# Which projections fill the waits of a delta-rule mixer: v's block before the banded attention, z's block in the scan

## The chip, the core and the metric

The kernel runs on one core of a Trainium2 chip. The metric is the device time of one execution in microseconds (us). Of the core's engines five appear below: TensorE (PE in the rows), VectorE (DVE), ScalarE (ACT), GpSimd (POOL) and SyncE (SP), which issues the loads.

## What the kernel computes

The program holds two blocks of a network for 256 tokens of width 1024, and the change lies in the first mixer of the second block. That mixer works on 272 rows (16 learned rows ahead of the 256 tokens, `N2` in the kernel). It projects them with one matrix, gives one part to a delta-rule mixer that runs over the sequence in both directions, and one part to a banded attention of 8 heads. Cut to what matters:

```python
def ab_mixer(u, w_in, ...):
    proj = u @ w_in
    qa, ka, va, za, ba, aa, qb, kb, vb = split_cols(proj, AB_SIZES)
    ya = delta_mixer(qa, ka, va, za, ba, aa, ...)
    yb = window_mixer(rmsnorm(qb), rmsnorm(kb), vb, sink)
    return concatenate([ya, yb]) @ w_out

def delta_mixer(hq, hk, hv, hz, hb, ha, conv_w, ...):
    q, k, v = split_cols(silu(centred_conv(concatenate([hq, hk, hv]), conv_w)), ...)
    q, k = l2norm(q), l2norm(k)                 # beta, g: gates of both directions
    fwd = gated_delta_chunked(q, k, v, beta_fwd, g_fwd)
    bwd = rev(gated_delta_chunked(rev(q), rev(k), rev(v), ...))
    return rmsnorm(fwd + bwd, o_gain) * silu(hz)

def gated_delta_chunked(q, k, v, beta, g):
    a_mat = where(strict, (k * beta) @ k.T * decay, 0)      # per chunk and head
    sol = triangular_solve(a_mat, [v * beta, k * beta * exp(gc)], unit_diagonal=True)
    def step(s, xs):                                        # the scan over chunks
        v_new = u_n - w_n @ s
        o = q_n @ s + qk_n @ v_new
        s = s * gl_n + k_n.T @ v_new
        return s, o
```

So v is wanted by the scan and not before it, and z only after the scan, in the last product. The triangular solve needs q, k and the gates, neither v nor z.

## The kernel before, in words

All work of the mixer is on one core. The 4 heads of the delta rule have keys and values of width 128; the sequence is cut into three pieces (16, 128 and 128 rows), and both directions run side by side. `delta` has four stages one after the other:

- the side rounds (`side`, L1575 to L1622): the norms of q and k, then `prepare`, which builds the decay masks, the scaled products and the rows of the gates for each piece and direction;
- the levels (`levels`): the triangular systems are inverted by doubling. `blocks` does four levels of 32x32 products (L1639), with a copy on ACT, a subtraction and a 32x32 transpose on DVE after each; `pairs` joins blocks to 64 and to 128 (L1678, L1685, L1688, L1695, L1700);
- the scan (`scan`, L1762 to L1801): three steps in each direction, matmuls of 128 columns with a copy or a product on ACT, POOL or DVE between them;
- `finish` (L1810, L1813), which norms the result and multiplies it by z; then the output projection.

Each stage is a chain over several engines, so PE would wait in it. The kernel therefore has filling work, written as a generator `fill`, and `spread(stage, fill, share)` takes `share` steps of it after each step of the stage: `SF` in the side rounds, `LF` in the levels, `CF` in the scan. What is left is run after the scan. The filling work consists of

- projections (`rest`): a block is 128 columns of the matrix over 272 rows. Its weights are split into a high and a low part (`wsplit`: a copy on ACT at L236, a subtraction on DVE at L267), and 24 matmuls of 272 columns follow (L272, L273, L274). Blocks 8 to 11 are v, 12 to 15 are z, 19 and 20 belong to the banded attention. A block of v ends in a short convolution (`conv_late`: L1314, L241 and four times L245 on DVE), a block of z in one product (L1395);
- the silu of v or z (`silu_exp`: three steps on ACT and one, L1307, on POOL) and `turned(vn, v)`, which transposes v by 12 matmuls (L297);
- the banded attention (`window`): two units for the learned rows and 16 of the heads (8 heads, two pieces of the rows; a head below is one such unit). It is a score (L1491, two records in the trace), a softmax on DVE and ACT, three transposes (L297) and products with the values (L1507).

The text of the program doesn't fix the order on an engine: a scheduler places the instructions from the order in which they are written, their costs and what they wait for. The rows of the section on the change are what it put out for either kernel.

Of the kernel before, what the change touches and what calls it, by code (L numbers as in the profile page):

```python
# [33 lines left out]
MORE = 2  # L34
PD = 2
PF = 5
LF = 4
WD = 2
SF = 1
CF = 4  # L40
VS = 0.7
WP = ()
ND = 2
OVER_AT = 4
# [102 lines left out]
def run(gen, n=None):  # L147

    while n is None or n > 0:
        if next(gen, gen) is gen:  # L150
            return
        n = None if n is None else n - 1
# [7 lines left out]
def spread(gen, fill, share):  # L160

    due = 0
    for _ in gen:
        due += share
        run(fill, int(due))
        due -= int(due)
# [14 lines left out]
class Kern:  # L181
# [1333 lines left out]
    def delta(self, c1, p1, pw, qk, v, z, qw, vba, rest, norms, qw_norms):  # L1515
# [38 lines left out]
        def turned(dst, x):  # L1554
            for t in (1, 2, 0):
                cc = self.hcols(t)
                n = cc.stop - cc.start
                b = self.bank()
                for h in range(4):
                    self.transpose(b[:n, h * 128:(h + 1) * 128], x[:, h, cc])  # L1560
                nc.scalar.copy(dst[:n, t], b[:n])
                yield
# [141 lines left out]
        def levels():  # L1704
            def through(d):
                yield from blocks(d)
                yield from pairs(d)

            return in_turn([through(0), through(1)])

        def side():
            yield from norms
            yield from flow([prepare(1, 0), prepare(1, 1), turned(kn, qk[:, 4:8])], PD)
            yield from flow([prepare(t, d) for t in (2, 0) for d in range(2)], PD)

        side = side()
        def values():
            yield from rest(pw, [8, 9, 10, 11])
            for h in range(4):
                self.silu_exp(pw, v[:, h], v[:, h])  # L1720
                yield
            yield from turned(vn, v)

        def filling():
            yield from rest(pw, [19, 20, 12, 13, 14, 15])
            yield from qw_norms(pw)
            due = 0
            for _ in self.window(c1, p1, pw, qw, vba, y):
                yield
                due += VS  # L1730
                while due >= 1:
                    run(vs, 1)
                    due -= 1
                    yield
            for h in range(4):
                self.silu_exp(pw, z[:, h], z[:, h])
                yield

        vs = values()
        y, fill = p1.tile([128, 4, N2], F32, name="yw"), filling()  # L1740
        spread(side, fill, SF)
        spread(levels(), fill, LF)
        run(vs)
        oT = v
        seen, st = set(), [None, None]
        def scan(step, d):
# [551 lines left out]
```

## Time and profile before

| | |
|---|---|
| median of 3 runs | 1607.31 us (1604.68 to 1607.84) |
| the profiled execution | 1608.48 us, of which the span of the profile is 1606.7 us |
| busy in the span | PE 1535.0, DVE 824.1, ACT 645.3, POOL 201.0 us |
| side rounds, last 44 us (917.0 to 961.4) | PE 42.73, DVE 33.62 us busy |
| levels (961.4 to 1017.7) | PE 50.40 of 56.3 us busy |
| scan (1017.7 to 1090.2) | PE 33.87 of the first 38.3 us, 34.18 of the other 34.2 us |

Times of stages are counted from the span's start. The granted clock is a column of the views: 1.00 is the upper level of TensorE's clock (2.4 GHz), 0.50 the lower one (1.2 GHz). A matmul at the lower level takes up to about twice as long, and PE then counts as busy for longer with the same work: a busy PE says nothing of its pace.

### The profile page before, as it was taken

The page shows a single profiled execution, that of the slowest core. Times are in us where ns is not written, and L with a number is a line of the kernel's source. Part 1 is how long each engine was busy: PE and PEld are TensorE (multiplying, and loading weights), DVE is VectorE, ACT ScalarE, POOL GpSimd, SP SyncE. Part 2 cuts the span into 40 slices and gives each one's busy share as a digit, 9 for nine tenths or more (in the row PEclk, how much of TensorE's full clock was granted, in tenths as well). Part 3 has the DMA queues.
Part 4 walks back from the last instruction along what each step waited for, and adds up shares of the span by engine and source line. Part 5 has one row for each costly group of instructions (what it writes and reads, how often), then busy time and mean ns, then how long its engine had stood idle before and what let it go on. Part 6 is the DMA issues. An engine that isn't in the chain of part 4 may idle for free.

```text
span 1606.7 us, 26861 instructions
## 1 busy us (share of the span) xinstructions
PE 1535.0 (96%) x10998; PEld 1170.3 (73%) x10998; DVE 824.1 (51%) x1624; ACT 645.3 (40%) x1309; POOL 201.0 (13%) x236
## 2 busy tenths in 40 slices
PE   7999999989799999998997899899999999999999
PEld 7788744444287876454436787588999998799998
DVE  6677612212345772131216776536666666576665
ACT  5466411111136642110115674545444455554443
POOL 0130100000101001000003631301111023220000
PEclk9999999999999999999999999689999999999999
DMA  8335899999462489999943111025555452254540
GB/s 348 140 131 186 338 407 421 380 421 421 145 239 71 159 315 356 422 382 419 421 206 140 66 54 56 1 83 191 173 184 184 157 192 79 79 180 164 184 156 27
DMA packets 50034, 348.77 MB, mean 217 GB/s; under 512 B 5616, under 2 KB 6896, under 8 KB 8688
## 3 DMA queue, kind: packets, MB, share of 16 engines
q1 hardware_dynamic: 49904, 346.97, 56.2%
q8 instruction: 90, 1.47, 0.4%
q14 instruction: 40, 0.33, 0.1%
HBM read 345.90 MB, written 1.05 MB: 216 GB/s over the span
## 4 chain that ended last, share of the span: by engine, by line
PE 45%; DVE 4%; ACT 2%; POOL 1%; issue 1%; DVEq 0%; POOLq 0%; ACTq 0%
PE bank L274 10%; PE bank L272 10%; PE bank L273 10%; PE bank L1033 3%; PE bank L1067 2%; DVE ring L267 1%; PE aux L1507 1%; PE aux L297 1%; PE bank L994 1%; PE aux L1491 1%; PE aux L2008 1%; PE bank L1639 1%; ACT ring L236 1%; PE bank L1769 1%; PE aux L1986 1%
## 5 line engine op out<-in xcount | busy, mean ns | idle before, releaser
L236 ACT ACTIVATE ring<-ring 128x1024 fp32r<-128x1024 f32 (+3 forms) x188 | 185.8, 994 | 188.6 <-PE bank L274 166.6
L267 DVE TENSOR_TENSOR ring<-ring,ring 128x1024 fp32r<-128x1024 f32 x145 | 180.4, 1244 | 93.5 <-ACT ring L236 93.1
L272 PE MATMUL bank<-uh,ring 128*128 128x272 f32 (+1 forms) x744 | 218.6, 294 | 2.3 <-ACT ring L236 2.3
L274 PE MATMUL bank<-uh,ring 128*128 128x272 f32 (+1 forms) x744 | 215.5, 290 | 4.2 <-DVE ring L267 3.7
L273 PE MATMUL bank<-ul,ring 128*128 128x272 f32 (+1 forms) x744 | 215.0, 289 | 0.0
L274 PEld LDWEIGHTS bank<-uh,ring 128*128 128x128 f32 x744 | 141.4, 190 | 6.0 <-DVE ring L267 5.6
L272 PEld LDWEIGHTS bank<-uh,ring 128*128 128x128 f32 x744 | 141.3, 190 | 5.1 <-ACT ring L236 2.5
L273 PEld LDWEIGHTS bank<-ul,ring 128*128 128x128 f32 x744 | 141.2, 190 | 0.9 <-issue 0.2
L274 PE MATMUL bank<-rh,ring 128*128 128x272 f32 (+1 forms) x496 | 141.6, 286 | 0.0
L272 PE MATMUL bank<-rh,ring 128*128 128x272 f32 (+1 forms) x496 | 141.4, 285 | 0.0
L273 PE MATMUL bank<-rl,ring 128*128 128x272 f32 (+1 forms) x496 | 140.9, 284 | 0.0
L1039 DVE TENSOR_TENSOR hid<-hid,bank 128x512 f32<-128x512 f32 x16 | 11.0, 687 | 186.4 <-PE bank L1033 173.7
L273 PEld LDWEIGHTS bank<-rl,ring 128*128 128x128 f32 x496 | 93.8, 189 | 0.0
L272 PEld LDWEIGHTS bank<-rh,ring 128*128 128x128 f32 x496 | 93.2, 188 | 0.0
L274 PEld LDWEIGHTS bank<-rh,ring 128*128 128x128 f32 x496 | 93.0, 187 | 0.0
L267 POOL TENSOR_TENSOR ring<-ring,ring 128x1024 fp32r<-128x1024 f32 x6 | 14.5, 2436 | 574.4 <-ACT ring L236 574.4
L1257 POOL TENSOR_TENSOR fr<-fr 128x272 f32<-128x272 f32 (+1 forms) x64 | 40.2, 629 | 287.3 <-DVE fr L245 283.4
L245 DVE SCALAR_TENSOR_TENSOR big<-bank,gs,big 128x512 fp32r<-128x512 f32 x32 | 24.0, 750 | 99.2 <-ACT big L236 97.5
L267 DVE TENSOR_TENSOR ring<-wsp,ring 128x1024 fp32r<-128x1024 f32 x41 | 52.8, 1287 | 26.1 <-ACT ring L236 26.1
L236 ACT ACTIVATE ring<-wsp 128x1024 fp32r<-128x1024 f32 x41 | 43.4, 1058 | 55.4 <-PE bank L274 54.2
L236 ACT ACTIVATE big<-bank,gs 128x512 fp32r<-128x512 f32 x32 | 22.0, 688 | 108.0 <-PE bank L1067 107.7
L994 PE MATMUL bank<-P,hnat 128*128 128x128 f32 x512 | 63.6, 286 | 0.0
(677 smaller groups left out, 3431.4 us busy)
## 6 DMA issues: line engine op xcount, KB each, us to landing
ring<-w_ff SPq DMA_DIRECT2D x50, 1024.0 KB, 4.9
ring<-w_down SPq DMA_DIRECT2D x34, 1024.0 KB, 12.9
ring<-w_up SPq DMA_DIRECT2D x30, 1024.0 KB, 13.0
ring<-w_gate SPq DMA_DIRECT2D x29, 1024.0 KB, 10.4
big<-w_gate SPq DMA_DIRECT2D x24, 1024.0 KB, 16.4
big<-w_up SPq DMA_DIRECT2D x18, 1024.0 KB, 10.9
big<-w_down SPq DMA_DIRECT2D x17, 1024.0 KB, 11.8
wsp<-w_ff SPq DMA_DIRECT2D x14, 1024.0 KB, 4.8
```

The source lines that it names most:

```text
L236: return self.nc.scalar.activation(out, in_, func, **kw)
L245: return (eng or self.nc.vector).scalar_tensor_tensor(out, in0, s, in1, op0=op0, op1=op1, **kw)
L267: (eng or self.nc.vector).tensor_sub(l, src, h.bitcast(F32))
L272: mm(out, lhs[0], rhs[0], start=first, stop=False)
L273: mm(out, lhs[0], rhs[1], start=False, stop=False)
L274: mm(out, lhs[1], rhs[0], start=False, stop=last)
L297: self.nc.tensor.transpose(out, in_, self.ident[:k, :k])
L994: mm(b[:, j * M2:(j + 1) * M2], h[:, t, (k + j) * 128:(k + j + 1) * 128], P[:, t], start=t == 0, stop=t == 1)
L1033: mm(b[e * 64:e * 64 + CAP], xg[:, k, e * CAP:(e + 1) * CAP], w[:, (2 * k + e) * 512:(2 * k + e + 1) * 512], start=k == 0, stop=k == 7)
L1067: mm(yb[n][e * 64:e * 64 + CAP], hT[:, k, e * 64:e * 64 + CAP], w[:, o:o + 512], start=k == 0, stop=k == 3)
L1257: nc.gpsimd.tensor_mul(r, r, r)
L1491: nc.tensor.matmul(b[:, :N2], qw[r, j, self.hcols(t)], qw[r, 4], start=True, stop=True)
```

## The change

Before, z's projections come first in the filling work, and v's projections, silu and transposes are mixed into the banded attention, 0.7 of a step after each of its steps; what is left of v is run before the scan, and z's silu comes last. In the change v's projections, silu and transposes come ahead of the banded attention. z's projections and silu (`last`) are mixed into the attention from its 20th step on (`ZN`), 0.6 of a step after each (`ZS`). The levels take 2 steps of filling for each of their own instead of 4 (`LF`). Ahead of the scan the filling is run until v is turned (`turns`), where before the rest of v was run.

```diff
--- before.py
+++ after.py
@@ -34,11 +34,11 @@
 MORE = 2
 PD = 2
 PF = 5
-LF = 4
+LF = 2
 WD = 2
 SF = 1
 CF = 4
-VS = 0.7
+ZN, ZS = 20, 0.6
 WP = ()
 ND = 2
 OVER_AT = 4
@@ -1714,33 +1714,37 @@
             yield from flow([prepare(t, d) for t in (2, 0) for d in range(2)], PD)
 
         side = side()
-        def values():
-            yield from rest(pw, [8, 9, 10, 11])
+        def filling():
+            yield from rest(pw, [19, 20, 8, 9, 10, 11])
+            yield from qw_norms(pw)
             for h in range(4):
                 self.silu_exp(pw, v[:, h], v[:, h])
                 yield
             yield from turned(vn, v)
-
-        def filling():
-            yield from rest(pw, [19, 20, 12, 13, 14, 15])
-            yield from qw_norms(pw)
-            due = 0
+            turns.append(True)
+            due, count = 0, 0
             for _ in self.window(c1, p1, pw, qw, vba, y):
                 yield
-                due += VS
+                due, count = due + (ZS if count >= ZN else 0), count + 1
                 while due >= 1:
-                    run(vs, 1)
+                    run(late, 1)
                     due -= 1
                     yield
+            yield from late
+
+        def last():
+
+            yield from rest(pw, [12, 13, 14, 15])
             for h in range(4):
                 self.silu_exp(pw, z[:, h], z[:, h])
                 yield
 
-        vs = values()
+        turns, late = [], last()
         y, fill = p1.tile([128, 4, N2], F32, name="yw"), filling()
         spread(side, fill, SF)
         spread(levels(), fill, LF)
-        run(vs)
+        while not turns:
+            next(fill)
         oT = v
         seen, st = set(), [None, None]
         def scan(step, d):
```

On DVE, in the last part of the side rounds, each block of projections is followed by its product or convolution. Before (names with their numbers; L1597, L1613 to L1615 are `prepare`, L267 is a split of weights):

```order
L1395 TENSOR_TENSOR z_6509<-bank_7080,nrs_6504 128x272
L1597 TENSOR_TENSOR dec_7128<-aux_7123,dec_7128 128x512
L267 TENSOR_TENSOR ring4_7205<-ring6_7083,ring4_7205 128x1024
L1597 TENSOR_TENSOR dec_7149<-aux_7144,dec_7149 128x512
L1613 TENSOR_TENSOR ring9_6980<-aux_7162,dec_7128 128x512
L1613 TENSOR_TENSOR wsp0_6984<-aux_7162,dec_7149 128x512
L1614 TENSOR_TENSOR dec_7128<-dec_7128,aux_7171 128x512
L1615 TENSOR_TENSOR ring1_6979<-aux_7161,dec_7128 128x512
L1614 TENSOR_TENSOR dec_7149<-dec_7149,aux_7183 128x512
```

And of the change, from the same place on:

```order
L1314 TENSOR_TENSOR dec_7122<-bank_7080,nrs_6504 128x272
L1597 TENSOR_TENSOR dec_7136<-aux_7131,dec_7136 128x512
L241 TENSOR_SCALAR v_6508<-dec_7122,ring5_6306 128x272
L267 TENSOR_TENSOR ring4_7221<-ring6_7083,ring4_7221 128x1024
L245 SCALAR_TENSOR_TENSOR v_6508<-dec_7122,ring5_6306,v_6508 128x272
L1597 TENSOR_TENSOR dec_7157<-aux_7152,dec_7157 128x512
L245 SCALAR_TENSOR_TENSOR v_6508<-dec_7122,ring5_6306,v_6508 128x272
L1613 TENSOR_TENSOR ring9_6980<-aux_7170,dec_7136 128x512
L245 SCALAR_TENSOR_TENSOR v_6508<-dec_7122,ring5_6306,v_6508 128x272
L1614 TENSOR_TENSOR dec_7136<-dec_7136,aux_7179 128x512
L245 SCALAR_TENSOR_TENSOR v_6508<-dec_7122,ring5_6306,v_6508 128x272
```

One product of z gives way to the six steps of a convolution of v; four such convolutions stand in the side rounds of the change, and one stood there before.

On PE, in the levels, before, where the first 32x32 products of a level stand (`ring_7826` is the split weights of one of v's blocks, `uh` and `ul` are the rows to be projected):

```order
L297 MATMUL aux<-prm,ws 16x128
L297 MATMUL aux<-prm,ws 128x128 x2
L1491 MATMUL aux<-qw 128x272 x2
L1639 MATMUL bank<-ring_6972,am 32x32 x11
L1639 MATMUL bank<-ring_6973,am 32x32 x36
L272 MATMUL bank<-uh,ring_7826 128x272
L273 MATMUL bank<-ul,ring_7826 128x272
L274 MATMUL bank<-uh,ring_7826 128x272
```

The levels of the change, at the second level:

```order
L1639 MATMUL bank<-qk,ring_6974 32x32 x72
L297 MATMUL bank<-prm,v 128x128 x2
L1639 MATMUL bank<-ring_6972,am 32x32 x21
L297 MATMUL bank<-prm,v 128x128
L1639 MATMUL bank<-ring_6972,am 32x32 x15
L1639 MATMUL bank<-ring_6973,am 32x32 x5
L297 MATMUL bank<-prm,v 128x128
L1639 MATMUL bank<-ring_6973,am 32x32 x31
L297 MATMUL bank<-prm,v 128x128 x4
L297 MATMUL bank<-prm,v 16x128 x4
```

No projection is left between the levels' products: before there are 72 from the first level to the last join. What the change has there instead are v's 12 transposes, 4 scores, and the products of 2 heads with their values (before: 8 and 6).

On PE, in the scan, before, at the end of its second step (`am`, `T`, `wsp`, `ring` hold operands of the scan, names with their numbers):

```order
L1491 MATMUL aux_8743<-qw_6510 128x272
L1491 MATMUL aux_8769<-qw_6510 128x272
L1781 MATMUL bank_8797<-am_8760,am_8795 128x128 x3
L1781 MATMUL bank_8804<-am_8767,T_6978 128x128 x4
L1796 MATMUL bank_8823<-qks_7360,am_8760 128x16 x4
L1796 MATMUL bank_8829<-wsp0_6984,am_8767 128x128 x4
L1762 MATMUL bank_8884<-ring1_6979 128x128 x4
L1762 MATMUL bank_8894<-wsp1_6983 128x128 x4
```

The scan of the change, in its first half (`ring4_8526` is the split weights of one of z's blocks):

```order
L1507 MATMUL aux_8441<-PTw_8410,vba_6355 64x128 x2
L1491 MATMUL aux_8478<-qw_6510 128x272
L1773 MATMUL bank_8554<-dec_8506,wsp1_6983 128x128 x2
L272 MATMUL bank_8521<-uh_6360,ring4_8526 128x272
L273 MATMUL bank_8521<-ul_6361,ring4_8526 128x272
L274 MATMUL bank_8521<-uh_6360,ring4_8526 128x272
...
L1785 MATMUL bank_8595<-am_8552,am_8593 128x128 x4
L1785 MATMUL bank_8602<-am_8559,T_6978 128x128 x2
L297 MATMUL aux_8490<-prm_64,ws_8468 16x128
L297 MATMUL aux_8490<-prm_64,ws_8468 128x128 x2
L1785 MATMUL bank_8602<-am_8559,T_6978 128x128 x2
L272 MATMUL bank_8521<-uh_6360,ring4_8526 128x272
L273 MATMUL bank_8521<-ul_6361,ring4_8526 128x272
L274 MATMUL bank_8521<-uh_6360,ring4_8526 128x272
```

All 96 projections of z now stand in the scan, in runs of 2, 4, 9, 9 and 18 and smaller ones after that, with 12 scores and the products of 14 heads (before: no projection, 8 and 10).

## Rows read from the trace of the kernel before

**Rows 1.** The page: span and instructions.

```profile
span 1606.7 us, 26861 instructions
```

**Rows 2.** Windows over the stages (head line names the columns; clock after POOL).

```profile
core 0: us, PE busy (x) PEld busy (x) DVE busy (x) ACT busy (x) POOL busy (x), PEclk, DMA share, GB/s
961.40:1017.70 56.30, 50.40 (x1550) 40.51 (x1547) 39.83 (x115) 26.22 (x81) 10.07 (x14) 0.92 0.12 41
1017.70:1056.00 38.30, 33.87 (x137) 25.02 (x137) 15.45 (x45) 16.82 (x51) 10.46 (x11) 0.51 0.00 1
1056.00:1090.20 34.20, 34.18 (x239) 27.32 (x237) 11.81 (x34) 15.38 (x46) 1.03 (x1) 0.95 0.36 124
```

**Rows 3.** DVE groups (count, busy us, mean ns) and two windows, side rounds.

```profile
L1395 DVE TENSOR_TENSOR z<-bank,nrs 128x272 f32<-128x272 f32 x4 | 1.8, 438 | 1.2 <-PE bank L274 1.2
L245 DVE SCALAR_TENSOR_TENSOR v<-dec,ring,v 128x272 f32<-128x272 f32 x3 | 1.4, 482 | 0.0
...
917.00:931.00 14.00, 13.97 (x101) 13.04 (x102) 9.42 (x19) 11.35 (x31) 2.22 (x5) 1.00 0.39 139
931.00:959.00 28.00, 26.36 (x217) 24.04 (x216) 21.79 (x41) 22.00 (x56) 9.16 (x15) 0.97 0.20 73
```

**Rows 4.** DVE group of the convolutions in the levels.

```profile
L245 DVE SCALAR_TENSOR_TENSOR v<-dec,ring,v 128x272 f32<-128x272 f32 x13 | 7.4, 571 | 0.0
```

**Rows 5.** PE groups in the levels, 961.4 to 1017.7.

```profile
L272 PE MATMUL bank<-uh,ring 128*128 128x272 f32 x24 | 8.4, 352 | 0.0
...
L1639 PE MATMUL bank<-ring,am 32*32 32x32 f32 x576 | 7.6, 207 | 2.4 <-issue 1.4 <-DVE wst L1464 1.1
...
L1700 PE MATMUL bank<-ring,qk 64*64 64x64 f32 x16 | 1.1, 221 | 0.0
...
L1678 PE MATMUL bank<-ring,wsp 32*32 32x32 f32 x32 | 0.7, 192 | 0.0
```

**Rows 6.** PE timeline at the lower clock: start, duration (us).

```profile
971.55 1.50 PE L1639 MATMUL bank<-ring,am 32*32 32x32 f32 x94
...
973.60 0.43 PE L274 MATMUL bank<-uh,ring 128*128 128x272 f32 x1
973.83 0.43 PE L272 MATMUL bank<-uh,ring 128*128 128x272 f32 x1
...
1023.85 0.85 PE L297 MATMUL aux<-prm,ws 128*16 128x128 f32 x3
1024.62 1.73 PE L1507 MATMUL aux<-PTw,vba 16*64 16x128 f32 x6
...
1030.01 1.27 PE L1491 MATMUL aux<-qw 64*128 64x272 f32 x2
```

**Rows 7.** PE timeline at the upper clock.

```profile
983.74 1.48 PE L1639 MATMUL bank<-ring,am 32*32 32x32 f32 x144
...
1060.30 0.72 PE L1491 MATMUL aux<-qw 64*128 64x272 f32 x2
...
1064.59 0.49 PE L297 MATMUL aux<-prm,ws 128*16 128x128 f32 x3
...
1066.28 1.01 PE L1507 MATMUL aux<-PTw,vba 16*64 16x128 f32 x6
...
1094.16 0.29 PE L274 MATMUL bank<-qw,ring 128*128 128x272 f32 x1
1094.28 0.29 PE L272 MATMUL bank<-qw,ring 128*128 128x272 f32 x1
```

**Rows 8.** Windows around the changes of the granted clock.

```profile
963.80:970.30 6.50, 4.14 (x284) 3.57 (x276) 5.76 (x19) 3.06 (x12) 1.69 (x4) 0.99 0.02 5
970.40:977.20 6.80, 6.80 (x132) 5.51 (x131) 3.72 (x12) 3.77 (x14) 2.29 (x3) 0.52 0.00 0
...
1025.00:1052.50 27.50, 26.50 (x102) 19.08 (x101) 9.69 (x30) 10.91 (x35) 9.18 (x10) 0.50 0.00 1
1052.50:1056.00 3.50, 3.50 (x18) 3.42 (x18) 0.00 (x0) 1.21 (x3) 0.00 (x0) 0.50 0.00 0
```

**Rows 9.** Waits of PE in the scan: total, times, longest (us).

```profile
PE bank L297 <- POOL v L1307: 3.4, 1, 3.4
```

## The prediction, made before the changed kernel ran

> **What bounds the kernel now.** I read four views in turn. The windows over the stages come first [rows 2]: PE is busy for 50.40 of 56.3 us in the levels and for 68.05 of 72.5 us in the scan, while no other engine passes 40 us in either. PE sets the end there, so what matters is how much PE work each stage holds and at which clock. The reader is to see the clock's column: the levels run at 0.92 in the mean, the first 38.3 us of the scan at 0.51, the rest at 0.95. Second, the PE timeline gives the price of each kind of work at both levels [rows 6, 7]: 144 products of 32x32 take 1.48 us at the upper level; at the lower one 94 take 1.50, so 144 take 2.3. Two neighbouring projections start 0.23 us apart at the lower level (973.60 and 973.83) and 0.12 at the upper (0.125 below, since several in a row stand that far apart). A score goes from 0.72 to 1.27 us, a head's three transposes from 0.49 to 0.85, its products with the values from 1.01 to 1.73. Third, narrower windows show what PE did before the clock moved [rows 8]. From 963.8 PE was busy for 4.14 of 6.5 us, mostly with 32x32 products, and from 970.4 the clock was 0.52. At the end of that low stretch stand projections, and the clock rose again. In the scan it stayed at 0.50 from 1025.0 to 1052.5 although PE was busy for 26.5 of the 27.5 us; after 18 matmuls of 128 columns without a gap (1052.5 to 1056.0) it rose. Fourth, the waits: PE stands for 3.4 us at the scan's front until v's silu is there [rows 9].
>
> **The change part by part.** The sum is made against the profiled execution, 1608.48 us with a span of 1606.7 [rows 1]; it lies 1.2 us above the median.
>
> *Side rounds.* DVE gets three more convolutions. One costs a product like z's (0.438), a scaling (taken as 0.4) and four L245 of 482 ns [rows 3], 2.75 us; four z products go (1.75). So +6.5 us on DVE. PE gets 20 projections fewer, -2.5 us. DVE is idle for 4.6 of the 14 us and 6.2 of the 28 us before the levels, PE for next to nothing. If all fits into DVE's gaps the stage ends as before; if none does, it is 6.5 us late. `prepare` needs only part of DVE at any time, so I take 0 and keep 0 to +6.5.
>
> The same four L245 have a mean of 571 ns in the levels, where they lie beside POOL's work [rows 4]. The Trainium skill, "SBUF — State Buffer", section "SBUF: two separate sides", says that a VectorE operation with two inputs in SBUF and a GpSimd operation that reads SBUF lock a shared pair of ports and the loser blocks wholly. That speaks against this move, since POOL is busy for 9.16 of those 28 us. By the two means a convolution would lose 4 x 0.09 = 0.4 us, 1 us in all; I leave it in the upper bound.
>
> *Levels.* 72 projections go [rows 5]: three blocks of 24. With them go 4 scores and the products of 4 heads; v's 12 transposes come. What then stands there, at the lower clock: 8 sets of 144 products, 18.4 us (8 x 2.3); 4 scores, 5.1; four groups of three transposes, 3.4; the products of two heads, 3.5; v's transposes at 0.28 each, 3.4. The joins of the pairs and the learned rows' scores are eleven groups of 0.7 to 1.8 us (the first and last kind, L1678 and L1700, are in [rows 5]), 10.4 us in all at the upper clock by that view and, at the ratio 1.7 of the other rows, 17.7 at the lower. These 51.5 us count the tail of each group beneath the next; the view's 24 groups add up to 68.7 us for 50.40 of busy time [rows 2, 5]. At the lower clock a tail is a smaller share, so I take 0.85, 43.8. To this come some 4 us of waits (5.9 before) and -2 us because the first 6 us, which before were at 0.99, stay so: 46 us instead of 56.3, **-10**. At the upper clock throughout, the same list is 11.8 + 2.9 + 2.0 + 2.0 + 2.0 + 10.4 = 31 us, by 0.85 some 27, and the waits for ACT and DVE between the products, no longer covered by projections, grow to some 9: 36 us, **-20**. Which of the two holds hangs on the clock. Before, it was the projections at 973.6 after which it rose; the levels of the change hold none, and their beginning is the stretch after which it fell. I take the lower level, -10, and keep -20 for the range.
>
> *Scan.* It takes what the levels gave up. 96 projections of z at 0.125, 12.0 us; 4 heads (0.72 + 0.49 + 1.01), 8.9; v's 12 transposes go, -2.0 at 0.163 each; the wait for v's silu goes, -3.4, since v is turned long before. That is +15.5 us if every piece ran at the clock it had. But the scan's first 37.5 us were at 0.51. Of these some 32 us were busy, and at the upper clock half of it, 16, would go. The question is when the projections lift the clock. In the order the first runs of z, 24 projections, fall in the first 13 us of the scan (counted at the lower clock); that is the sort of work after which it rose at 977. If it rises there, 13 us at the lower clock are left, which cost 6.5 of the 16: 15.5 - 16 + 6.5 = **+6**. If these short runs between gaps don't lift it and only the run of 18 does, about where it rose before, the scan loses all 16 again and, with z's work and the added heads partly at the lower clock, 3 more: 15.5 + 3, **+18.5**.
>
> The loads: the second half of the matrix is z's instead of v's, issued at the same place of SP's queue; one piece of the output matrix is now issued behind the split of z's last block, some 20 us ahead of its use, and costs nothing. Without that cover it would be one landing. z's silu (ACT and POOL) now follows at the scan's end; POOL has 1.03 us to do in the last 34.2 [rows 2]. I take nothing, and name it as a rival.
>
> The sum: 0 - 10 + 6 = -4, **1604.5 against 1608.48, and 1603.3 against the median**.
>
> **The rivals.** *The late clock (slower).* All of the levels at the lower clock, as forecast, and the rise in the scan only with the run of 18: -10 + 18.5 = +8.5, **1616**. For it speaks that a PE busy for 26.5 of 27.5 us stayed at 0.50; against it that the 12 projections at the end of the low stretch at 970.4 were enough before. It decides from a rise later than some 20 us into the scan, where the sum is 0.
>
> *The clock stays up in the levels (faster).* If v's transposes, 128 columns wide and set among the products, hold or lift it, the levels take 36 us and the scan starts at the upper level: -20 + 15.5 - 16 = -20.5, **1587**. The Trainium skill, "TensorE: Matmul & The Clock Gate", section "Part 1: The HAM clock gate (the "warmup" mystery)", says that the throttled clock is the default and activity releases it. By that, a PE kept busier with fewer waits should be released sooner, which is this rival; the trace agrees only in part, since the busy stretch at 1025.0 stayed at 0.50 [rows 8].
>
> *The wait moves from v to z (no change).* The last z block's silu comes after the scan's last rounds, and the product with z at L1813 waits as long as v's did, 3.4 us [rows 9]: -4 + 3.4, **1606.7**. Against it stands an idle POOL.
>
> **How the numbers follow.** Forecast 0.35, late clock 0.32, clock up 0.15, no change 0.10, and 0.08 for the DVE of the side rounds losing its cover (+3 to +6 over the forecast). About 0.2% (3.2 us) is what a measurement of this kernel can tell from no change. The forecast lies just beyond it: two thirds of its chance count as faster, the rest as same. Faster: 0.15 + 0.24, near 0.40; same: 0.10 + 0.11, 0.22; slower: 0.32 + 0.06, 0.38. The range goes from 1590 to 1617, leaving out most of the fast rival and the end of the slow one; the forecast alone would be 1600 to 1609.
>
> **What would show it.** Right: the first 32x32 product within 2 us of 961.4; the last L1700 near 1007 with a clock near 0.5 from 970 on; no PE wait for v; the clock back at 1.00 within 15 us of the scan's start; the scan 78 to 79 us long. Wrong: a levels stage at 1.00 and 36 us long, or a scan over 85 us with the clock at 0.50 beyond 30 us, or a wait at L1813 on POOL.

## The result, and the profile after

The changed kernel took 1617.21 us (median of 8 runs, 1611.94 to 1626.76), the kernel before 1605.41 us: a ratio of 1.0077, with a 95% interval of 1.005 to 1.0104. The change makes the kernel slower by some 12 us, where 1603.3 and a gain were forecast; 1617.21 lies just outside the range. That it lies beside the 1616 of the rival with the late clock is luck, as the stages show below.

The profiled execution was the longest of the eight, with a span of 1625.0 us. The windows over its stages answer to [rows 2, 3, 8] (columns as there). The stretch from 952.5 is the end of the side rounds, from 969.0 the levels, from 1017.2 the scan; 1054.2 is where its clock rises:

```profile
931.00:952.50 21.50, 20.07 (x165) 19.29 (x163) 20.38 (x32) 13.81 (x28) 8.67 (x10) 1.00 0.29 99
952.50:969.00 16.50, 10.00 (x55) 5.02 (x55) 12.85 (x30) 10.54 (x35) 3.91 (x7) 0.59 0.00 1
969.00:1017.20 48.20, 40.88 (x1431) 33.50 (x1431) 27.17 (x78) 20.72 (x62) 15.01 (x18) 0.64 0.07 26
1017.20:1054.20 37.00, 36.81 (x144) 28.64 (x145) 13.58 (x35) 10.01 (x32) 3.83 (x4) 0.50 0.00 0
1054.20:1110.00 55.80, 55.17 (x371) 43.37 (x370) 23.06 (x65) 27.79 (x82) 3.76 (x4) 0.94 0.28 95
```

Three things are to be seen. The side rounds end in 16.5 us in which PE is busy for 10 and the clock is 0.59. The levels last 48.2 us in place of 56.3, at a mean clock of 0.64 in place of 0.92. The scan lasts 92.8 us in place of 72.5, with PE busy for 99% of it, and its first 37 us are wholly at the lower level.

Those 20 us of the scan are mostly moved work, not clock. An estimate from the rows is length times clock, what a stage would take at the upper level throughout, and the rest of its length, what the clock withheld. By it the scan holds 71.0 full-speed us where it held 52.0, and the clock withheld 21.8 us where it withheld 20.5. The levels gave up 51.8 - 30.8 = 21.0 full-speed us, but what the clock withheld there rose from 4.5 to 17.4. So in this profile the new loss of clock lies in the levels and at the end of the side rounds; the scan did not win back what the forecast had it win.

The PE timeline at the end of the side rounds (a bracket is the idle time before and what ended it):

```profile
951.83 0.29 PE L274 MATMUL bank<-uh,ring 128*128 128x272 f32 x1
951.95 0.60 PE L297 MATMUL aux<-prm,dt 128*128 128x128 f32 x4
955.16 1.03 PE L1355 MATMUL aux<-dsq,c 128*128 128x272 f32 x2 [2.61 <-DVE dec L1614]
956.77 1.28 PE L1355 MATMUL aux<-dsq,c 128*128 128x272 f32 x2 [0.58 <-ACT dsq L236]
...
960.87 1.27 PE L1355 MATMUL aux<-dsq,c 128*128 128x272 f32 x2 [1.42 <-ACT dsq L236]
...
969.02 1.18 PE L1639 MATMUL bank<-ring,am 32*32 32x32 f32 x72 [1.02 <-DVE ring L1643]
```

The last projection of the side rounds starts at 951.83. Then PE waits 2.6 us for `prepare`'s L1614, and at 955 the clock falls: the pair of L1355 that took 0.70 us in the kernel before takes 1.28. The kernel before has a fall at this place too, behind a wait of 1.46 us, but with fewer waits after it the clock is back at 964 there:

```profile
955.56 0.70 PE L1355 MATMUL aux<-dsq,c 128*128 128x272 f32 x2
...
958.05 1.27 PE L1355 MATMUL aux<-dsq,c 128*128 128x272 f32 x2 [1.46 <-ACT dsq L236]
```

```profile
957.00:964.00 7.00, 5.92 (x116) 2.43 (x120) 5.63 (x12) 2.90 (x10) 5.62 (x6) 0.51 0.01 2
964.00:970.40 6.40, 4.04 (x271) 3.43 (x257) 5.56 (x18) 3.17 (x12) 1.69 (x4) 1.00 0.02 5
```

In the change it stays down until 982, 13 us into the levels. What made L1614 late stands on DVE and POOL in the same microseconds:

```profile
944.95 1.21 DVE L267 TENSOR_TENSOR ring<-ring,ring 128x1024 fp32r<-128x1024 f32 x1
...
949.51 1.36 DVE L245 SCALAR_TENSOR_TENSOR v<-dec,ring,v 128x272 f32<-128x272 f32 x1
950.79 2.29 DVE L267 TENSOR_TENSOR ring<-ring,ring 128x1024 fp32r<-128x1024 f32 x1
953.01 0.49 DVE L245 SCALAR_TENSOR_TENSOR v<-dec,ring,v 128x272 f32<-128x272 f32 x1
...
954.43 0.67 DVE L1614 TENSOR_TENSOR dec<-dec,aux 128x512 f32<-128x512 f32 x1
```

```profile
949.29 1.28 POOL L1533 TENSOR_TENSOR ring<-ring,qk 128x512 f32<-128x512 f32 x1 [0.82 <-ACT ring L236]
...
950.53 1.47 POOL L1533 TENSOR_TENSOR wsp<-wsp,qk 128x512 f32<-128x512 f32 x1
```

DVE has no gap here. Its L245 of 0.49 takes 1.36 us and a split of 1.21 takes 2.29, each in the time in which POOL's product runs. By groups, over 917 to 969 us:

```profile
L245 DVE SCALAR_TENSOR_TENSOR v<-dec,ring,v 128x272 f32<-128x272 f32 x16 | 10.9, 683 | 0.0
L267 DVE TENSOR_TENSOR ring<-ring,ring 128x1024 fp32r<-128x1024 f32 x7 | 9.6, 1372 | 2.0 <-ACT ring L236 2.0
```

An L245 of v has a mean of 683 ns, where [rows 3] had 482; a split 1372 ns, which in the kernel before (917.0 to 961.4) was 1222:

```profile
L267 DVE TENSOR_TENSOR ring<-ring,ring 128x1024 fp32r<-128x1024 f32 x7 | 8.6, 1222 | 3.8 <-ACT ring L236 3.8
```

From the first L1355 of the stage to the first 32x32 product the kernel before takes 45.7 us (915.7 to 961.4), the changed one 51.4 (917.6 to 969.0): +5.7. With -8.1 in the levels, +20.3 in the scan, +1.9 ahead of the stage and -1.5 behind the scan, that is the 18.3 us between the two spans.

### The profile page after: what moved, and what is told of

The parts are those of the page before. It is cut to its first block, busy times and chain, and to the rows that moved or that the text cites. A ratio compares the mean times of both kernels' runs of the same rounds, so it can differ in the third digit from the quotient of the medians.

```text
span 1625.0 us, 26875 instructions
## 1 busy us (share of the span) xinstructions
PE 1549.3 (95%) x10998; PEld 1182.5 (73%) x10998; DVE 828.7 (51%) x1624; ACT 644.8 (40%) x1309; POOL 202.4 (12%) x236
## 4 chain that ended last, share of the span: by engine, by line
PE 44%; DVE 5%; ACT 2%; issue 2%; POOL 1%; DVEq 0%; POOLq 0%; ACTq 0%
PE bank L274 9%; PE bank L272 9%; PE bank L273 9%; PE bank L1033 3%; PE bank L1067 2%; PE aux L1507 1%; DVE ring L267 1%; PE aux L297 1%; PE aux L1491 1%; PE bank L1639 1%; PE bank L994 1%; PE aux L2012 1%; ACT ring L236 1%; PE bank L297 1%; PE aux L1355 1%
## 5 line engine op out<-in xcount | busy, mean ns | idle before, releaser
L267 DVE TENSOR_TENSOR ring<-ring,ring 128x1024 fp32r<-128x1024 f32 x145 | 181.1, 1250 | 92.2 <-ACT ring L236 91.8
L272 PE MATMUL bank<-uh,ring 128*128 128x272 f32 (+1 forms) x744 | 220.6, 297 | 2.3 <-ACT ring L236 2.3
L274 PE MATMUL bank<-uh,ring 128*128 128x272 f32 (+1 forms) x744 | 217.9, 293 | 5.0 <-DVE ring L267 4.8
L274 PEld LDWEIGHTS bank<-uh,ring 128*128 128x128 f32 x744 | 143.3, 193 | 8.1 <-DVE ring L267 7.0
L272 PEld LDWEIGHTS bank<-uh,ring 128*128 128x128 f32 x744 | 143.4, 193 | 3.7 <-ACT ring L236 2.5
L267 POOL TENSOR_TENSOR ring<-ring,ring 128x1024 fp32r<-128x1024 f32 x6 | 14.5, 2433 | 574.5 <-ACT ring L236 574.5
L245 DVE SCALAR_TENSOR_TENSOR big<-bank,gs,big 128x512 fp32r<-128x512 f32 x32 | 24.0, 751 | 99.1 <-ACT big L236 97.5
L267 DVE TENSOR_TENSOR ring<-wsp,ring 128x1024 fp32r<-128x1024 f32 x41 | 52.5, 1280 | 26.1 <-ACT ring L236 26.1
```

The source lines that it names most:

```text
L245: return (eng or self.nc.vector).scalar_tensor_tensor(out, in0, s, in1, op0=op0, op1=op1, **kw)
L267: (eng or self.nc.vector).tensor_sub(l, src, h.bitcast(F32))
L272: mm(out, lhs[0], rhs[0], start=first, stop=False)
L274: mm(out, lhs[1], rhs[0], start=False, stop=last)
```

## The experiments

Times are medians; a ratio is against the kernel before on the same chip. The last two columns are medians over a kernel's runs too: the mean granted clock, and the time less (1 - clock) x span, that is the time less the full-speed microseconds that the clock did not grant. The first row takes the runs of the kernel before that were made beside the experiments.

| run | median us | ratio, 95% interval | clock | less what the clock withheld |
|---|---|---|---|---|
| before (74 runs) | 1605.2 | | 0.972 | 1559.8 |
| the change (8 and 6 runs) | 1617.3 | 1.0077 (1.005 to 1.0104), 1.0088 (1.0058 to 1.0117) | 0.9645 | 1559.3 |
| e1_dense | 1610.62 | 1.0038 (1.0023 to 1.0053) | 0.970 | 1562.2 |
| e2_noconv | 1613.48 | 1.0059 (1.0038 to 1.0079) | 0.963 | 1555.6 |
| d1_both | 1607.79 | 1.0009 (0.9993 to 1.0025) | 0.968 | 1557.0 |
| e3_lf4 | 1609.30 | 1.0029 (1.0012 to 1.0047) | 0.972 | 1562.9 |
| e5_before_lf2 | 1628.43 | 1.013 (1.0101 to 1.016) | 0.961 | 1565.6 |
| e4_zn0 | 1611.94 | 1.003 (1.0016 to 1.0045) | 0.969 | 1562.0 |
| e6_dense4 | 1621.01 | 1.0081 (1.0065 to 1.0096) | 0.963 | 1561.1 |
| b2_z_front | 1611.63 | 1.0029 (1.0016 to 1.0042) | 0.969 | 1562.0 |
| c1_z12_side | 1617.01 | 1.0088 (1.0062 to 1.0115) | 0.965 | 1560.7 |
| c2_before_lf5 | 1603.23 | 0.9991 (0.9975 to 1.0006) | 0.972 | 1558.1 |
| c3_lf6 | 1620.89 | 1.0083 (1.0056 to 1.011) | 0.964 | 1563.5 |

By the last column the change and the kernel before agree within 0.5 us, so the 12 us go with the clock: the change adds no work and removes none. The column is an estimate that also counts waits at the lower level as clock, and it doesn't say which stage lost; smaller differences can cancel in it (without the convolutions, e2_noconv, it is 3.7 us lower).

**a0_again: the changed kernel once more.** No edit.

> The changed kernel once more, for a second profile and a time on the same chip as the runs beside it. Its profiled execution was the longest of eight (1626.76 against a median of 1617.21). If the place at which the clock rises in the scan is fixed by the order, this profile shows it again near 37 us into the scan (scan 92 us); if that place differs between executions, this one shows an earlier rise and a scan of some 80 us.

Median 1619.24 (1608.98 to 1625.59), the profiled run 1616.79. This run is close to the median of all 14. Side rounds and levels are much as in the first profile (51.4 and 50.3 us), but the scan takes 82.8 us, since its clock rises after 22 us:

```profile
965.40:1015.70 50.30, 41.59 (x1431) 34.04 (x1431) 27.35 (x79) 20.74 (x62) 14.96 (x17) 0.64 0.08 25
1015.70:1038.00 22.30, 22.11 (x88) 16.83 (x89) 7.90 (x20) 4.67 (x17) 3.07 (x3) 0.52 0.00 1
1038.00:1098.50 60.50, 59.87 (x426) 47.58 (x426) 28.53 (x81) 33.16 (x98) 4.53 (x5) 1.00 0.26 88
```

The same order of instructions, and another place. Its PE timeline in the second run of 9 projections, where the spacing falls from 0.23 to 0.13 us within the run:

```profile
1036.60 0.43 PE L274 MATMUL bank<-uh,ring 128*128 128x272 f32 x1
1036.82 0.43 PE L272 MATMUL bank<-uh,ring 128*128 128x272 f32 x1
...
1037.41 0.29 PE L272 MATMUL bank<-uh,ring 128*128 128x272 f32 x1
1037.53 0.29 PE L273 MATMUL bank<-ul,ring 128*128 128x272 f32 x1
1037.66 0.28 PE L274 MATMUL bank<-uh,ring 128*128 128x272 f32 x1
```

The last line is the 24th projection of the scan, 22 us behind its start.

In the first profile of the change that run passed at the lower level and the clock rose only at the end of the run of 18 (1050.62 to 1054.5):

```profile
1037.53 0.57 PE L272 MATMUL bank<-uh,ring 128*128 128x272 f32 x1
...
1039.49 0.43 PE L274 MATMUL bank<-uh,ring 128*128 128x272 f32 x1
...
1054.16 0.41 PE L272 MATMUL bank<-uh,ring 128*128 128x272 f32 x1
1054.39 0.32 PE L273 MATMUL bank<-ul,ring 128*128 128x272 f32 x1
```

At which place of the same order it rises differs between executions. The two profiles differ by 10.0 us in span, and 10.0 us is what their scans differ by; the 14 runs spread from 1608.98 us at a mean clock of 0.969 to 1626.76 at 0.957.

**e1_dense: two blocks of z in one stretch at the scan's front.**

```diff
         while not turns:
             next(fill)
+        run(late, 8)
```

> The change with the projections of two of z's blocks (run(late, 8)) brought in one stretch to the front of the scan; the work is the same. Theory A, the clock (short runs of projections between gaps leave it at the lower level, a long run lifts it): the clock is back within 10 us of the scan's start, the scan falls from 92.8 us to some 76, and the kernel is 10 to 17 us faster than the change, 1600 to 1607. Theory B, the work alone (the scan got longer because it took over z's projections and four heads): the scan's chain now starts 6 us later behind 48 projections and the time is the same as the change or up to 6 us longer, 1617 to 1623.

1610.62 us, 7 less than the change, with all of its work, and 3.6 above theory A's 1600 to 1607. The profile is of its fastest run (1608.71): the clock is back 3 us into the scan, within a run of 11 projections, and the scan takes 77.3 us:

```profile
1013.20:1016.50 3.30, 3.30 (x18) 3.18 (x19) 2.26 (x4) 0.52 (x2) 0.00 (x0) 0.62 0.00 0
1016.50:1090.50 74.00, 72.51 (x496) 56.89 (x494) 34.93 (x96) 37.25 (x112) 7.11 (x8) 0.98 0.21 72
```

Theory B is out: the same work in another order costs 7 us less. The early rise that theory A forecast came, its gain not in full. The 48 projections stand in front of the scan's chain, whose first matmul starts 17 us into the scan; that this is what the rest of the gain went into was not tested here. Side rounds and levels stayed as long as in the change (51.4 and 48.8 us).

**e2_noconv: v's convolution left out.**

```diff
-                    self.conv_late(pw, b, rs, cw[:, i], v[:, i - 8])
+                    nc.vector.tensor_mul(v[:, i - 8], b, rs)
```

> The change with v's convolution left out: one product on DVE per block in place of six steps, so that the side rounds hold no more work on DVE than before; the result is that of another v. If the three added convolutions on DVE make the side rounds longer (theory C), the first 32x32 product falls from 969.0 back to 961 to 962 us and the kernel gains 7 us over the change; if the scheduler's other order on PE does it, it stays at 966 or later.

1613.48 us, 4 less than the change and not the 7 expected; its six runs spread over 13 us, so the times alone hardly tell the two apart (the intervals of the ratios overlap). The stage's length does: in its profile (of its fastest run, 1605.60) the first L1355 to the first product takes 47.4 us (913.7 to 961.1), where the change took 51.4 in both of its profiles. So 4.0 of the 5.7 us that the side rounds grew by are the convolutions'. The clock falls nevertheless, at 951 us, after a wait for another of L1355's inputs:

```profile
951.86 1.28 PE L1355 MATMUL aux<-dsq,c 128*128 128x272 f32 x2 [3.38 <-ACT dsq L236]
```

So theory C holds for most of the length, and not for the clock.

**d1_both: the edits of e1_dense and e2_noconv together** (v's convolution is left out here too).

> The change with both suspected losses taken away at once: v's convolution left out (one product per block; the result is that of another v) and two of z's blocks in one stretch at the scan's front. Apart, the two gained 4 to 5 us (1613.5) and 7 to 8 us (1610.6) on the change's 1617 to 1619. If they are the two halves of its loss and do not overlap, together they give 1604 to 1608, the time of before; if both only shift the same stretch of lower clock, the sum is not reached and it stays at 1609 to 1613.

1607.79 us, no longer told from before (1.0009, 0.9993 to 1.0025). Apart they gave 6.7 and 3.8 us against the 1617.3 of all runs of the change, together 9.5 of the 12: the sum is nearly reached, as the first of the two expectations has it. That rests on the times of 12 runs. The profile is of a long one (1611.85), whose scan still takes 82.3 us, so it doesn't show the two losses gone stage by stage.

**c1_z12_side: one of z's blocks in the last side rounds.**

```diff
-            yield from rest(pw, [19, 20, 8, 9, 10, 11])
+            yield from rest(pw, [19, 20, 8, 9, 10, 11, 12])
...
-            yield from rest(pw, [12, 13, 14, 15])
+            yield from rest(pw, [13, 14, 15])
```

> The change with one of z's blocks (12) projected in the side rounds, behind v's projections and ahead of v's silu, so that the last rounds have projections on PE again as in the kernel before; v's four convolutions stay there, and 24 projections fewer are left for the scan. Theory D (the clock falls at 953 us because the last side rounds have no projections left, and is still down in the levels): PE's waits between 952 and 969 shrink, the clock falls later than 955, and the kernel is 4 to 8 us faster than the change, 1609 to 1613. Theory C (DVE's convolutions make the rounds late whatever PE has): the first 32x32 product stays 51 us behind the first L1355, as in the change, and the clock falls at the same place; 1614 to 1620.

1617.01 us: nothing gained. The clock does hold until 958 in place of 955, but the first product comes 53 us after the first L1355, no sooner. DVE is busy for 25.89 of the first 27 us, which fits theory C, though PE's waits there are for ACT as well:

```profile
931.00:958.00 27.00, 24.33 (x195) 22.76 (x194) 25.89 (x43) 16.30 (x32) 8.82 (x12) 1.00 0.23 79
958.00:970.00 12.00, 7.53 (x42) 3.91 (x42) 8.57 (x20) 8.63 (x29) 4.78 (x6) 0.52 0.00 0
```

**e3_lf4: the new order with the levels' old share of filling.**

```diff
-LF = 2
+LF = 4
```

> The change with four steps of filling in the levels, as before, instead of two. More of the attention and 57 of z's projections come into the levels and their end, 39 remain for the scan. Theory A: the projections near the end of the levels, one run of 14 and runs of 9 to 12 before it, lift the clock near the scan's start, the scan falls to 55 to 65 us while the levels grow by 8 to 12; in all 8 to 15 us faster than the change, 1602 to 1609. Theory B: the work only moves between the stages, within 3 us of the change.

1609.30 us, at the upper end of theory A. With the order moved and `LF` left alone the loss is 4 us; `LF` 2 adds the other 8. (The profiled run, 1620.2, is one of its longest; the median is of 12.)

**e5_before_lf2: the other half alone**, `LF` 2 in the kernel before.

> The kernel before with two steps of filling in the levels instead of four, the other part of the change alone. The levels get shorter by 5 to 9 us; 36 projections of v now stand in one run ahead of the scan, followed by the wait for v's silu. Theory A: that run brings the upper clock to the scan's start, and unless the wait behind it lets it fall again the scan gains more than the work that moves there costs: 1598 to 1605. Theory B: the moved work costs in the scan what the levels save, and the wait for v grows: 1605 to 1612.

1628.43 us, 22 more than before and beyond what either theory gave. So `LF` 2 costs 22 us in the old order and 8 in the new one. The windows from the end of the levels on, and PE's longest waits there:

```profile
1014.10:1024.00 9.90, 9.90 (x41) 7.83 (x42) 2.29 (x5) 1.56 (x6) 0.00 (x0) 0.51 0.00 0
1024.00:1030.00 6.00, 5.07 (x34) 3.85 (x32) 5.87 (x16) 2.33 (x5) 1.04 (x1) 1.00 0.00 0
1030.00:1062.00 32.00, 27.18 (x112) 21.12 (x112) 12.69 (x35) 15.75 (x46) 10.94 (x12) 0.52 0.00 1
```

```profile
PE bank L297 <- POOL v L1307: 4.1, 2, 2.7
PE bank L1769 <- POOL dec L1533: 1.6, 1, 1.6
```

The 36 projections of v ahead of the scan lift the clock at 1024, as theory A has it; then PE waits for v's silu (2.7 and 1.4 us), the clock falls again at 1030 and stays down for 32 us. What the run had lifted did not outlast the next wait.

**b2_z_front: two blocks of z held back in the kernel before,** to stand between v's silu and its transposes (with a load of their own).

```diff
                 self.silu_exp(pw, v[:, h], v[:, h])
                 yield
+            yield from rest(pw, [14, 15])
             yield from turned(vn, v)
...
-            yield from rest(pw, [19, 20, 12, 13, 14, 15])
+            yield from rest(pw, [19, 20, 12, 13])
```

> The kernel before, with z's blocks 14 and 15 alone held back: their 48 projections stand between v's silu and v's transposes, as a run of 30 and more ahead of the scan, where the kernel before waits 3.4 us for that silu and its clock falls. The levels keep v's projections between their products, the side rounds keep z's light products. Theory A (a long run of projections lifts or holds the clock, short ones don't): the scan runs at the upper clock from its start, some 60 to 64 us instead of 72.4, and the kernel is 6 to 12 us faster than before, 1593 to 1599. Theory B (PE's work alone counts): the work only moves, no change within 3 us, or 3 us faster by the covered wait.

1611.63 us, 5 slower than before: theory A's forecast fails here. The upper clock is there at the scan's front (it rose at 1026, behind a run of 12 projections ahead of the long one), but a wait of 2.2 us for the attention's softmax follows at its end, and it is down again for 21 us:

```profile
1027.70:1046.00 18.30, 15.36 (x104) 11.49 (x104) 12.38 (x35) 11.68 (x38) 3.52 (x5) 1.00 0.08 35
1046.00:1067.00 21.00, 20.69 (x84) 15.79 (x85) 5.34 (x17) 4.70 (x15) 5.71 (x6) 0.52 0.00 1
```

```profile
PE aux L297 <- DVE wst L1467: 2.2, 1, 2.2
```

**e4_zn0, e6_dense4, c3_lf6, c2_before_lf5: other shares.** `LF` 4 with `ZN` 0 in the change (z's projections in the levels); `run(late, 16)` in place of the 8 of e1_dense; `LF` 6 in the change; `LF` 5 in the kernel before.

> The change with z's projections mixed in from the attention's first step (ZN 0) and four steps of filling in the levels: v early as in the change, and projections, now z's, in the levels and at the scan's front. The side rounds keep the four convolutions. If the change loses by the clock in the scan (some 7 us) and by the side rounds (some 5), this one gets the first back and keeps the second: levels 55 to 60 us, scan 62 to 70, 1605 to 1611. If v's place were the trouble as such, it stays at 1615 to 1620.

> The change with all four of z's blocks brought in one stretch to the scan's front (run(late, 16)), 96 projections with a few of the attention's matmuls between. With two blocks there the clock was back 3 us into the scan, but fell again for 3 us at 1036, and the median was 1610.6. If the clock alone sets the rest of the loss, this one is the same, 1607 to 1613; if the scan's chain waits behind the stretch, 6 us of it are added, 1614 to 1619.

> The change with six steps of filling in the levels: two gave 1617 to 1619, four 1609.3. The attention and all of z's projections are done by the end of the levels, with runs of projections between the products from the third level on, and the scan has nothing left to fill but three heads. Theory A: levels of some 75 us mostly at the upper clock, a scan of 55 us with waits in it, in which the clock falls; 1605 to 1612. If the clock holds in the scan as well: 1598 to 1603.

> The kernel before with five steps of filling in the levels. With two it was 22 us slower than with four, for the clock fell in the levels and twice in the scan. If more filling work in the levels means a higher clock there and less work at the lower clock in the scan, it gains: 1597 to 1603. If the levels have no waits left to fill, the work only moves and the wait for v's silu ends inside the levels: 1603 to 1608. I lean to the second.

e4_zn0 (1611.94) missed its upper end by 1 us; its profile, of a run of 1604.34, has levels of 61.7 us at 0.86 and a scan of 57.7 at 0.94, and the side rounds' 51.4 us unchanged. e6_dense4 (1621.01) is worse than e1_dense by 10 and beyond both of its ranges; in its profile the clock fell once more at 1046 for 21 us. c3_lf6 (1620.89) missed by 9: its levels last 90.2 us. c2_before_lf5 (1603.23) can't be told from before. No version here is clearly faster than the kernel before.

## Why the prediction was wrong

The forecast took the span to change by 0 (side rounds), -10 (levels) and +6 (scan). The profile near the median (a0_again, 1616.79) has +5.7, -6.0 and +10.3, the longest run has +5.7, -8.1 and +20.3.

**The step that failed is the scan's clock:** "If it rises there, 13 us at the lower clock are left", and with it the +6. The 24 projections, in runs of 2, 4, 9 and 9, do not end 13 us into the scan: with the scan's own matmuls and the attention's between them, at the lower level, they end after 22 us in one profile and 22.7 in the other. In the profile near the median they do lift the clock, within the last run of 9, so the mechanism came true there and its place was 9 us too late: +10.3. In the longest run they did not lift it at all, it rose at 37 us with the run of 18, and the scan cost +20.3. That is the rival with the late clock, which had +18.5, by the row that shows a PE busy for 26.5 of 27.5 us at 0.50 [rows 8]. I gave that row less weight than the projections at 973.6, which were 12 in one piece. That rival's 1616 is beside the median by chance: of the two runs that were profiled, its late rise came only in the one of 1626.76, and the one near the median got there by other terms. That the order of the same work decides when the scan's clock rises is shown by e1_dense.

**The side rounds were mis-sized, by as much:** 0 was taken out of 0 to +6.5, and +5.7 measured in both profiles. The argument from DVE's idle time (6.2 of 28 us) was wrong in two ways. The idle time was not where the convolutions came, and they grew dearer there: a mean of 683 ns in place of 482 for an L245. e2_noconv puts 4.0 us of it on the convolutions; the other 1.7 weren't taken apart. The Trainium skill ("SBUF — State Buffer", "SBUF: two separate sides") has a VectorE operation with two inputs in SBUF and a GpSimd operation that reads SBUF lock a shared pair of ports against each other for a whole instruction, and it spoke against this move. The trace agrees here: an L245 of 1.36 us in place of 0.49 and a split of 2.29 in place of 1.21, each beside one of POOL's products. I had priced it at 1 us and left it in the bound.

**The levels were right in kind and 2 to 4 us short:** -8.1 and -6.0 against -10, at a mean clock of 0.64, with the lower level for most of it as forecast. Two things were not. The -2 for a start at the upper level rested on a row that begins at 963.8; the levels begin at 961.4, at the lower clock, and in the change the clock had fallen in the last side rounds (at 952 and 955) and was down for their first 13 us. And the rival in which v's transposes lift the clock came for a moment: in the first profile it rose at the last eight in a row, and fell again behind a wait of 2.5 us between the products. A set of 144 products takes 1.59 us right behind the transposes and 2.14 after that wait:

```profile
980.57 1.97 PE L297 MATMUL bank<-prm,v 128*128 128x128 f32 x8
982.47 1.59 PE L1639 MATMUL bank<-qk,ring 32*32 32x32 f32 x144
...
989.65 0.36 PE L1639 MATMUL bank<-ring,am 32*32 32x32 f32 x9 [2.50 <-issue]
...
996.68 2.14 PE L1639 MATMUL bank<-ring,am 32*32 32x32 f32 x144
```

**No wait for v was left, and none for z came in its place** in the scan, whose PE was busy for 99%; z's loads cost nothing that the trace shows.

What stays open: why the rise comes within the second run of 9 projections in one execution and at the end of the run of 18 in another; how much of the 8 us of `LF` 2 falls to each stage, for which no profile near e3_lf4's median was taken; and the 2.6 us between d1_both and before, which is no more than these runs can tell apart.

## What to carry to other kernels

Where the clock is low for tens of microseconds, price a move of filling work by the clock that each stage will have, and look first at the waits of two or three microseconds that the move opens: in the profiles of before, of the change, of e5_before_lf2 and of b2_z_front one such wait was followed by 20 us or more at half the pace (one of 1.46 us, in before, by 7). Work out when the filling work comes at the pace that the stage has: 24 projections that were counted at 13 us came at 22. Filling work in small pieces hides waits, but it was no sure way back to the upper clock; a wait behind a long run undid what the run had gained (e5_before_lf2, b2_z_front). Idle time of an engine is cover only at the place where the added instructions come, and beside a busy POOL they weren't at their usual price here.

## What the runs showed of the hardware

Time and clock go together from execution to execution. The 14 runs of one program range over 1.1%, with mean clocks of 0.957 to 0.969, and one profile of it can lie 9 us from the median. Eight runs of each side gave an interval of half a per cent, and the profile that one reads should be set beside the clocks of the other runs first: read alone, the first profile of the change puts 10 us more on the scan than the run near the median does.
